# Delta net inversion: block masks laid on A instead of on its product, ScalarE evicting the product, and k, q, kb kept in the load's buffer

## Chip, cores and metric

One core of a Trainium2 chip runs the whole program once. The metric is the device time of that execution in microseconds; the median of several runs is compared.

## What is computed

One decoder layer: x (1024 tokens by 1024 features) is normed and projected; a gated delta net (4 heads of 128) and a sparse attention (8 heads of 64) run side by side, their outputs are merged, and a gated feed-forward part follows. All is float32. The change lies in the delta net, whose chunks need the inverse of a unit lower triangular matrix:

```python
kb = k * beta[..., None]
a_low = jnp.where(strict, jnp.einsum('bhnid,bhnjd->bhnij', kb, k) * decay, 0.0)
ia = a_low + jnp.eye(c, dtype=q.dtype)
u = lax.linalg.triangular_solve(ia, v * beta[..., None], left_side=True, lower=True, unit_diagonal=True)
w = lax.linalg.triangular_solve(ia, kb * jnp.exp(gc)[..., None], left_side=True, lower=True, unit_diagonal=True)
...
def step(state, inp):
    qk_n, qg_n, kd_n, u_n, w_n, gl_n = inp
    v_new = u_n - jnp.einsum('bhcd,bhde->bhce', w_n, state)
    o_n = jnp.einsum('bhcd,bhde->bhce', qg_n, state) + jnp.einsum('bhij,bhje->bhie', qk_n, v_new)
    state = state * gl_n[..., None, None] + jnp.einsum('bhcd,bhce->bhde', kd_n, v_new)
```

## The kernel before

The sequence is cut into 8 chunks of 128 tokens; a tile `[128, 4, 128]` holds one chunk for the 4 heads. After the projections to q, k, v (until some 205 us) four generators run woven into each other, with the remaining input projections as filler:

- `prepare_chunks` loads a chunk's q, k, v as `G` (line 506, SP's queue, one buffer) and the summed decays as `E` (line 509). TensorE transposes v, k and q (`pvt`, `pk`, `pqt`, lines 522, 530, 536). VectorE subtracts on `E` (line 513), GpSimd applies two selects to it (lines 514 and 516), ScalarE takes the exponential. GpSimd's `rr` (line 541) gives the norms, and VectorE scales to `kh` and `qh` (544, 546); GpSimd makes `kb` and `kd` and, in two products, `KQs` (helper `pmul`, line 89). TensorE transposes `kh`, `qh`, `kb` (555, 560, 565) and forms `pa` (580), from which VectorE makes `A` and `qkT` (583, 584). `A` goes to DRAM as `sq_a` (587) and comes back as 16x16 diagonal blocks `U` (591); VectorE inverts these in 15 small steps of a product `Ut` (596) and a sum `Yb` (598); they go to DRAM as `sq_y` (599) and come back as the block diagonal `Y` (601).
- `solve_chunks` widens the inverse three times, to blocks of 32, 64 and 128 (levels 4 to 6). A level transposes `Y` (`px`, 616), copies it to `X` (ScalarE, 617), forms `pp` from `A` and `X` (621), keeps only the off-diagonal blocks by multiplying with the mask `LM` (`Pm`, VectorE, 623), forms `py` (627) and subtracts it from `Y` (VectorE, 628).
- `scan_chunks` carries the state from chunk to chunk (`pr`, `pvn`, `pS`, `po`, `zt`), and `turn_chunks` transposes and splits its output (`at`, line 86).
- The filler is `projections`: three matmuls for each step (lines 147 to 149, `pn` and `pm`), evicted by ScalarE (`nst`, 710, two PSUM buffers).

`weave` picks the next piece by a small model of TensorE's time, in which each yield gives its cost and its delay. TensorE's instructions stay in that order by `manual_schedule`; on the other engines and the queues the framework's scheduler sets the order. The small tiles lie in a pool where a name has one buffer if no number is given: `gt("A", ..., 3)`, `gt("X", ...)`, `gt("Pm", ...)`.

Of the kernel before, what the change touches and what calls it, by code (L numbers as in the profile page):

```python
# [15 lines left out]
ALU = mybir.AluOpType  # L16
# [4 lines left out]
P = 128  # L21
# [4 lines left out]
H = 4  # L26
# [7 lines left out]
def tile_hybrid(ctx: ExitStack, tc: tile.TileContext, a: dict, out: bass.AP, dbg=None):  # L34
    nc = tc.nc
# [43 lines left out]
    def blocks(t):  # L79
        return bass.AP(tensor=t.tensor, offset=t.offset, ap=[[16 * P + 16, 32], [P, 16], [1, 16]])  # L80
# [7 lines left out]
    def pmul(out_, x, y):  # L88
        nc.gpsimd.tensor_tensor(out_, x, y, op=ALU.mult)
# [206 lines left out]
    def psB(name):  # L296
        return ps.tile([P, H, P], F32, tag="pb", name=name, bufs=3)
# [75 lines left out]
    def gt(name, shape, bufs=1, dt=F32):  # L373
        return gpool[0].tile(shape, dt, tag=name, name=name, bufs=bufs)
# [8 lines left out]
                            fill=0.0, base=0, channel_multiplier=-1)  # L383
# [5 lines left out]
    LM = gt("LM", [P, 3, P])  # L389
    for l in range(4, 7):  # L390
        b = 1 << l
        nb = P // (2 * b)
        v = LM[:, l - 4, :].rearrange("p (m s) -> p m s", s=2 * b)
        src = ones.rearrange("p (m s) -> p m s", s=2 * b)

        nc.gpsimd.affine_select(out=v, in_=src, pattern=[[-2 * b, nb], [0, 2 * b]], compare_op=ALU.is_ge,
                                fill=0.0, base=-b, channel_multiplier=1)

        nc.gpsimd.affine_select(out=v, in_=v, pattern=[[2 * b, nb], [0, 2 * b]], compare_op=ALU.is_gt,
                                fill=0.0, base=2 * b, channel_multiplier=-1)  # L400

        nc.gpsimd.affine_select(out=v, in_=v, pattern=[[0, nb], [-1, 2 * b]], compare_op=ALU.is_gt,
                                fill=0.0, base=b, channel_multiplier=0)
    Yb = [gt(f"Yb{i}", [32, 16, 16]) for i in range(2)]
    for i in range(2):
        nc.vector.memset(Yb[i], 0.0)
# [81 lines left out]
    def bc(ap, n=P):  # L488
        return ap[:, :, None].broadcast_to([P, ap.shape[1], n])

    def bc_h(ap):
        return ap[:, None, :].broadcast_to([P, H, P])
# [8 lines left out]
    def prepare_chunks():  # L501
        for c in range(NT):
            while c >= scanned[0] + 3:
                yield None
            G = gt("G", [P, 12, P])
# [9 lines left out]
                                    fill=NEG, base=0, channel_multiplier=-1)  # L515
            nc.gpsimd.affine_select(out=E, in_=E, pattern=[[0, H], [1, P]], compare_op=ALU.not_equal,
                                    fill=0.0, base=0, channel_multiplier=-1)
# [22 lines left out]
            rr = gt("rr", [P, 24], 2)[:, :8]  # L540
            nc.gpsimd.tensor_tensor(rr, ss, expo, op=ALU.pow)
            yield 230, 5000
            kh = gt("kh", [P, H, P])
            nc.vector.tensor_tensor(kh, pk, bc(rr[:, 0:4]), op=ALU.mult)
            qh = gt("qh", [P, H, P])
            nc.vector.tensor_tensor(qh, pq, bc(rr[:, 4:8]), op=ALU.mult)
            kb = gt("kb", [P, H, P])
            pmul(kb, kh, bc(beta[:, c, :]))
            yield 0, 3500

# [23 lines left out]
            A = gt("A", [P, H, P], 3)  # L574
            qkT = gt("qkT", [P, H, P], 3)
            for u in range(2):
                pa = psA("pa")
                pav = pa.rearrange("p (h u) i -> p h u i", h=2)
                for h in range(2):
                    nc.tensor.matmul(pav[:, h, :, :], khT[:, 2 * u + h, :], KQ[:, 2 * u + h, :, :],  # L580
                                     start=True, stop=True)
# [11 lines left out]
            for j in range(14, -1, -1):  # L593
# [3 lines left out]
                                        yb[:, j + 1:, j + 1:].rearrange("p b c -> p c b"), op=ALU.mult)  # L597
                nc.vector.tensor_reduce(yb[:, j, j + 1:], t[:, :n, :n], axis=AX.X, op=ALU.add, negate=True)
            nc.sync.dma_start(blocks(sq_y[c % 2]), yb)
# [6 lines left out]
    def solve_chunks():  # L606
        for c in range(NT):
            while begun[0] <= c:
                yield None
            yield 0, max(0.0, begun_at[c] + 21000 - m.t["pe"])  # L610
            A, Y = chunk[c][4], chunk[c][6]
            for l in range(4, 7):
                X = gt("X", [P, H, P])
                pt = psB("px")
                for h in range(H):
                    nc.tensor.transpose(pt[:, h, :], Y[:, h, :], ident)
                nc.scalar.copy(X, pt)
                yield 230, EV
                pp = psB("pp")
                for h in range(H):  # L620
                    nc.tensor.matmul(pp[:, h, :], A[:, h, :], X[:, h, :], start=True, stop=True)
                Pm = gt("Pm", [P, H, P])
                nc.vector.tensor_tensor(Pm, pp, bc_h(LM[:, l - 4, :]), op=ALU.mult)
                yield 880, EV
                py = psB("py")
                for h in range(H):
                    nc.tensor.matmul(py[:, h, :], Pm[:, h, :], Y[:, h, :], start=True, stop=True)
                nc.vector.tensor_tensor(Y, Y, py, op=ALU.subtract)
                yield 880, EV
            solved[0] = c + 1  # L630
# [97 lines left out]

    rest = projections()
    weave(m, [steps(m, g) for g in (scan_chunks(), turn_chunks(), solve_chunks(), prepare_chunks())], steps(m, rest))  # L730
    gd.close()

# [30 lines left out]
    for mask, pat, op, base, mult in ((maskD, -1, ALU.is_ge, 0, 1), (maskE, 1, ALU.is_gt, 0, -1),  # L763
# [3 lines left out]
                                channel_multiplier=mult)  # L767
# [5 lines left out]
                            fill=0.0, base=-31, channel_multiplier=1)  # L773
# [169 lines left out]
    with ExitStack() as ph:  # L943
        ap_ = pool(ph, "attn")

        def at_(name, shape, bufs=1, dt=F32):
            return ap_.tile(shape, dt, tag=name, name=name, bufs=bufs)
# [77 lines left out]
        def scores():  # L1025
            for u, (i, g, br, j0, nk) in enumerate(units):
# [10 lines left out]
                if br == 0:  # L1037
# [4 lines left out]
                    for h in range(4):  # L1042
                        for l in range(2):
                            nc.tensor.matmul(sv[:, h, :], qt[:, h, l, :], KCS[:, g, :], start=l == 0, stop=False)
                        nc.tensor.matmul(sv[:, h, :], identb, maskC[:, 56 - 8 * i:120 - 8 * i], start=False, stop=True)
                    nc.vector.tensor_reduce(mx[:, :, 0], sv, axis=AX.X, op=ALU.max, negate=True)
                    pr = at_("Pc", [P, 4, 64], 2)
# [7 lines left out]
                else:  # L1055
                    b = 0 if br == 1 else 1
                    cuts = (0, w) if nk <= 4 else (0, (nk + 1) // 2 * P, w)
                    for n in range(len(cuts) - 1):
# [7 lines left out]
                        for h in range(4):  # L1066
# [10 lines left out]
                            for e, (m0, mk) in enumerate(ext):  # L1077
                                nc.tensor.matmul(s[:, m0:m0 + P], identb, mk, start=False, stop=e == len(ext) - 1)  # L1078
                            nc.vector.tensor_reduce(mx[:, h, n:n + 1], s, axis=AX.X, op=ALU.max, negate=True)  # L1079
                            nc.scalar.activation(pr, s, AF.Exp, bias=mx[:, h, n:n + 1], accum_out=sums[:, h, n:n + 1])  # L1080
# [115 lines left out]
    A, Aop = {}, {}  # L1196
# [497 lines left out]
```

## Time and profile before

| | |
|---|---|
| median of 3 runs | 1787.52 us (1783.7 to 1788.48) |
| profiled execution | 1787.32 us |
| its span, first to last instruction | 1785.6 us |
| TensorE busy | 1717.4 us, 96% |
| VectorE busy | 1093.7 us, 61% |
| ScalarE busy | 767.2 us, 43% |
| GpSimd busy | 625.5 us, 35% |

The profile page gives busy time by engine and the span in 40 slices; the trace gives each instruction with its start, its length and what ended the idle time before it. PE is TensorE, PEld its weight loads, DVE is VectorE, ACT is ScalarE, POOL is GpSimd, SPq is SP's transfer queue. An idle time is put down to the instruction that came last. The woven stretch runs from about 225 to 510 us.

### The profile page before, as it was taken

The numbers are of one execution on the slowest core, as the hardware profiler recorded it, in microseconds if no ns is written. First come the engines' busy times: TensorE is split into PE (matmuls) and PEld (weight loads), VectorE is DVE, ScalarE is ACT, GpSimd is POOL, SyncE is SP. The second block draws the span as 40 slices with busy tenths as digits, with TensorE's granted clock in tenths as the row PEclk, the third lists the DMA queues.
The fourth block names the chain that finished last, engine by engine and source line by source line (L and its number), as shares of the span: only waits on it lengthen the run. The fifth ranks groups of instructions, "written<-read, shape, count | busy, mean of one in ns | idle before, by whom it ended". The sixth has DMA issues, their size and how long they took to land.

```text
span 1785.6 us, 25989 instructions
## 1 busy us (share of the span) xinstructions
PE 1717.4 (96%) x9348; PEld 1455.3 (82%) x9348; DVE 1093.7 (61%) x2062; ACT 767.2 (43%) x1806; POOL 625.5 (35%) x919
## 2 busy tenths in 40 slices
PE   7999988989999999999999999899999999999998
PEld 7888888989878777777878888688888888878886
DVE  6466556565534578677754434665555555588685
ACT  5244433343321598777742222433333333344452
POOL 3400143444131666667540220644435434200000
PEclk9999989999999999999999999999999999999999
DMA  6332443433364412011138360033333333482342
GB/s 209 95 101 95 144 118 108 111 100 100 94 173 141 112 42 54 22 48 36 51 108 249 114 212 1 12 119 107 100 95 121 103 99 112 161 306 88 98 139 100
DMA packets 183009, 196.39 MB, mean 110 GB/s; under 512 B 23409, under 2 KB 139361, under 8 KB 182881
## 3 DMA queue, kind: packets, MB, share of 16 engines
q1 hardware_dynamic: 164112, 162.03, 29.8%
q0 software_dynamic: 18560, 32.62, 6.1%
q8 instruction: 73, 1.20, 0.3%
q14 instruction: 56, 0.45, 0.1%
q10 hardware_dynamic: 208, 0.09, 0.0%
HBM read 139.01 MB, written 55.69 MB: 109 GB/s over the span
## 4 chain that ended last, share of the span: by engine, by line
PE 78%; issue 6%; DVE 6%; POOL 4%; ACT 2%; DMA 2%; POOLq 0%; SPq 0%; DVEq 0%; ACTq 0%
PE M L149 14%; PE M L148 14%; PE M L147 14%; PE ppt L1133 3%; PE s L1075 3%; PE pq L147 2%; PE pq L149 2%; PE pq L148 2%; PE po L1160 2%; PE pm L147 2%; PE pm L148 2%; PE pm L149 2%; PE po L1161 2%; DVE Ut L596 1%; PE pn L147 1%
## 5 line engine op out<-in xcount | busy, mean ns | idle before, releaser
L86 DVE TENSOR_TENSOR ptl<-ppt,pth 128x512 fp32r<-128x512 f32 (+1 forms) x148 | 98.8, 683 | 36.0 <-ACT pth L85 35.0
L1110 POOL TENSOR_SCALAR Ps<-Ps,cs 128x384 f32<-128x384 f32 (+3 forms) x192 | 112.3, 603 | 13.0 <-DVE cs L1088 6.0
L85 ACT ACTIVATE ahi<-fraw 128x512 fp32r<-128x512 f32 x88 | 55.6, 632 | 141.7 <-PE M L148 141.7
L1080 ACT ACTIVATE Ps<-s,mx 128x384 f32<-128x384 f32 (+3 forms) x192 | 106.5, 563 | 16.6 <-DVE mx L1079 15.6
L1079 DVE TENSOR_REDUCE mx<-s 128x1 f32<-128x384 f32 (+3 forms) x192 | 95.3, 514 | 22.8 <-PE s L1078 20.4
L1075 PE MATMUL s<-KT,qt 128*128 128x384 f32 (+3 forms) x384 | 100.4, 359 | 2.9 <-ACT Ps L1080 1.8
L147 PE MATMUL pn<-whi,h 128*128 128x264 f32 (+1 forms) x320 | 100.7, 315 | 0.0
L147 PE MATMUL pm<-h,whi 128*128 128x512 f32 x224 | 96.6, 431 | 0.8 <-ACT thm L725 0.7
L85 ACT ACTIVATE pth<-ppt 128x512 fp32r<-128x512 f32 (+1 forms) x148 | 86.2, 603 | 24.6 <-PE ppt L1133 23.6
L149 PE MATMUL pn<-whi,h 128*128 128x264 f32 (+1 forms) x320 | 91.6, 286 | 0.0
L148 PE MATMUL pn<-wlo,h 128*128 128x264 f32 (+1 forms) x320 | 91.5, 286 | 0.0
L149 PE MATMUL pm<-h,wlo 128*128 128x512 f32 x224 | 88.5, 395 | 0.0
L85 ACT ACTIVATE ahi<-fsum 128x512 fp32r<-128x512 f32 x66 | 41.7, 632 | 108.1 <-PE M L148 106.1
L148 PE MATMUL pm<-h,whi 128*128 128x512 f32 x224 | 88.1, 393 | 0.0
L86 DVE TENSOR_TENSOR wlo<-wraw,whi 128x1024 fp32r<-128x1024 f32 (+1 forms) x50 | 61.1, 1231 | 41.1 <-ACT whi L85 39.4
L86 DVE TENSOR_TENSOR alo<-fraw,ahi 128x512 fp32r<-128x512 f32 x88 | 70.5, 801 | 23.8 <-ACT ahi L85 23.8
L1617 POOL TENSOR_TENSOR rms_r<-rms_ms,small 128x1 f32<-128x1 f32 x8 | 5.1, 646 | 226.6 <-DVE rms_ms L1615 226.6
L1133 PE MATMUL ppt<-ident,Ps 128*128 128x128 f32 x528 | 77.7, 274 | 1.1 <-POOL Ps L1110 1.1
L147 PE MATMUL M<-act,ahi 128*128 128x512 f32 x194 | 76.1, 392 | 1.8 <-ACT act L85 1.8
L148 PE MATMUL M<-act,ahi 128*128 128x512 f32 x194 | 76.4, 394 | 0.3 <-DVE act L86 0.3
L149 PE MATMUL M<-act,alo 128*128 128x512 f32 x194 | 76.1, 392 | 0.0
L147 PE MATMUL pq<-h,whi 128*128 128x512 f32 x192 | 74.7, 389 | 0.0
(518 smaller groups left out, 5444.8 us busy)
## 6 DMA issues: line engine op xcount, KB each, us to landing
wraw<-in_w_in_dram SPq DMA_DIRECT2D x50, 512.0 KB, 4.4
fraw<-in_w_gate_up_dram SPq DMA_DIRECT2D x44, 512.0 KB, 4.2
ar<-act_d SPq DMA_DIRECT2D x35, 512.0 KB, 3.5
act_d<-asum SPq DMA_DIRECT2D x44, 256.0 KB, 2.4
act_d<-act SPq DMA_DIRECT2D x33, 256.0 KB, 2.0
gt_d<-thm POOLq DMA_DIRECT2D x32, 256.0 KB, 2.8
gg<-gt_d SPq DMA_DIRECT2D x32, 256.0 KB, 2.9
qkv_d<-ac POOLq DMA_DIRECT2D x24, 256.0 KB, 2.3
```

What stands on the lines that cost most here:

```text
L85: nc.scalar.activation(hi, src, AF.Copy)
L86: nc.vector.tensor_tensor(lo, src, hi.bitcast(F32), op=ALU.subtract)
L147: nc.tensor.matmul(ps, ah, bh, start=first, stop=False)
L148: nc.tensor.matmul(ps, ah, bl, start=False, stop=False)
L149: nc.tensor.matmul(ps, al, bh, start=False, stop=last)
L1075: nc.tensor.matmul(s, qt[:, h, l, :], KT[g][:, b, j0 * P + c0:j0 * P + c1], start=l == 0, stop=l == 1 and not ext)
L1079: nc.vector.tensor_reduce(mx[:, h, n:n + 1], s, axis=AX.X, op=ALU.max, negate=True)
L1080: nc.scalar.activation(pr, s, AF.Exp, bias=mx[:, h, n:n + 1], accum_out=sums[:, h, n:n + 1])
L1110: nc.gpsimd.tensor_scalar(v, v, cs[:, h, n:n + 1], 1.0, op0=ALU.mult, op1=ALU.mult)
L1133: nc.tensor.transpose(pt[:k, h, :], prs[h][:, jj * P:jj * P + k], ident)
L1160: nc.tensor.matmul(po, v, th_, start=first, stop=False)
L1161: nc.tensor.matmul(po, v, tl_, start=False, stop=fin is not None)
```

## The change

The mask tables `LM` are turned (the block rows and columns that they keep change places), and VectorE multiplies `A` by the mask into a new tile `Am` with two buffers at the head of each level. `pp` is formed from `Am`, and ScalarE copies it to `Pm`. `kh`, `qh` and `kb` lose their tiles and are written over q, k and v in `G`.

```diff
@@ the masks
-                                fill=0.0, base=-b, channel_multiplier=1)
+                                fill=0.0, base=0, channel_multiplier=1)
...
-                                fill=0.0, base=2 * b, channel_multiplier=-1)
-
-        nc.gpsimd.affine_select(out=v, in_=v, pattern=[[0, nb], [-1, 2 * b]], compare_op=ALU.is_gt,
-                                fill=0.0, base=b, channel_multiplier=0)
+                                fill=0.0, base=b, channel_multiplier=-1)
+
+        nc.gpsimd.affine_select(out=v, in_=v, pattern=[[0, nb], [1, 2 * b]], compare_op=ALU.is_ge,
+                                fill=0.0, base=-b, channel_multiplier=0)
@@ prepare_chunks
-            kh = gt("kh", [P, H, P])
+            kh, qh, kb = (G[:, 4 * j:4 * j + 4, :] for j in range(3))
             nc.vector.tensor_tensor(kh, pk, bc(rr[:, 0:4]), op=ALU.mult)
-            qh = gt("qh", [P, H, P])
             nc.vector.tensor_tensor(qh, pq, bc(rr[:, 4:8]), op=ALU.mult)
-            kb = gt("kb", [P, H, P])
             pmul(kb, kh, bc(beta[:, c, :]))
@@ solve_chunks
             for l in range(4, 7):
+                Am = gt("Am", [P, H, P], 2)
+                nc.vector.tensor_tensor(Am, A, bc_h(LM[:, l - 4, :]), op=ALU.mult)
                 X = gt("X", [P, H, P])
...
-                    nc.tensor.matmul(pp[:, h, :], A[:, h, :], X[:, h, :], start=True, stop=True)
+                    nc.tensor.matmul(pp[:, h, :], Am[:, h, :], X[:, h, :], start=True, stop=True)
                 Pm = gt("Pm", [P, H, P])
-                nc.vector.tensor_tensor(Pm, pp, bc_h(LM[:, l - 4, :]), op=ALU.mult)
+                nc.scalar.copy(Pm, pp)
```

TensorE's order is the same in both. On VectorE, the start of a chunk's small inversion (the stretch at 355 us of the trace). Before:

```order
L513 TENSOR_TENSOR E<-E,gc 128x512
L596 TENSOR_TENSOR Ut<-U,Yb_880 32x1
L598 TENSOR_REDUCE Yb_880<-Ut 32x1
L623 TENSOR_TENSOR Pm<-pp,LM 128x512
L596 TENSOR_TENSOR Ut<-U,Yb_880 32x2x2
L598 TENSOR_REDUCE Yb_880<-Ut 32x2
L596 TENSOR_TENSOR Ut<-U,Yb_880 32x3x3
```

And with the change (lines from 547 on stand two lower, so that 596 is 594):

```order
L513 TENSOR_TENSOR E<-E,gc 128x512
L594 TENSOR_TENSOR Ut<-U,Yb_880 32x1
L596 TENSOR_REDUCE Yb_880<-Ut 32x1
L612 TENSOR_TENSOR Am<-A,LM 128x512
L594 TENSOR_TENSOR Ut<-U,Yb_880 32x2x2
L596 TENSOR_REDUCE Yb_880<-Ut 32x2
L594 TENSOR_TENSOR Ut<-U,Yb_880 32x3x3
```

`Am` stands in the slot that `Pm` had; the first two `Am` of the program stand ahead, so each is the one of two levels later.

On VectorE, the end of the same small inversion (at 368 us). Before:

```order
L598 TENSOR_REDUCE Yb_880<-Ut 32x15
L539 SCALAR_TENSOR_TENSOR ss<-ss,rscale 128x8
L623 TENSOR_TENSOR Pm<-pp,LM 128x512
L544 TENSOR_TENSOR kh<-pk,rr 128x512
L546 TENSOR_TENSOR qh<-pqt,rr 128x512
L86 TENSOR_TENSOR at_3840<-pat,at_3839 128x512
L628 TENSOR_TENSOR Y<-Y,py 128x512
L623 TENSOR_TENSOR Pm<-pp,LM 128x512
```

With the change (`kh` and `qh` are now parts of `G`):

```order
L596 TENSOR_REDUCE Yb_880<-Ut 32x15
L539 SCALAR_TENSOR_TENSOR ss<-ss,rscale 128x8
L612 TENSOR_TENSOR Am<-A,LM 128x512
L544 TENSOR_TENSOR G<-pk,rr 128x512
L545 TENSOR_TENSOR G<-pqt,rr 128x512
L86 TENSOR_TENSOR at_3847<-pat,at_3846 128x512
L628 TENSOR_TENSOR Y<-Y,py 128x512
L612 TENSOR_TENSOR Am<-A,LM 128x512
```

`Am` again takes `Pm`'s place, and `Y` keeps its place behind `kh`, `qh` and `at`.

On SP's queue, around the load of a later chunk's `G` (at 381 to 394 us). Before:

```order
L587 DMA sq_a_106<-A 128x4x128
L509 DMA E<-gc_d 128x512
L591 DMA U<-sq_a_106 32x16x16
L506 DMA G<-qkv_d_73 128x12x128
L599 DMA sq_y_108<-Yb_880 32x16x16
L680 DMA zt<-z_d_77 128x512
L601 DMA Y<-sq_y_108 128x4x128
L587 DMA sq_a_107<-A 128x4x128
```

With the change:

```order
L589 DMA U<-sq_a_106 32x16x16
L597 DMA sq_y_108<-Yb_880 32x16x16
L680 DMA zt<-z_d_77 128x512
L599 DMA Y<-sq_y_108 128x4x128
L506 DMA G<-qkv_d_73 128x12x128
L585 DMA sq_a_107<-A 128x4x128
L509 DMA E<-gc_d 128x512
L589 DMA U<-sq_a_107 32x16x16
```

The load of `G` moves from behind `U` to in front of the next chunk's `sq_a` and `E`.

## Rows read from the trace of the kernel before

**Rows 1.** What TensorE waited for, 225 to 510 us: total us, times, longest.
```profile
PE py L627 <- DVE Pm L623: 11.3, 8, 2.2
PE px L616 <- DVE Y L628: 4.0, 4, 1.4
```
**Rows 2.** Groups by line, 225 to 510 us: busy us, mean ns, idle us before.
```profile
L623 DVE TENSOR_TENSOR Pm<-pp,LM 128x512 f32<-128x512 f32 x24 | 16.3, 679 | 30.7 <-PE pp L621 30.7
L513 DVE TENSOR_TENSOR E<-E,gc 128x512 f32<-128x512 f32 x7 | 4.8, 692 | 17.1 <-ACT sb L512 17.1
L617 ACT COPY X<-px 128x512 f32<-128x512 f32 x24 | 14.0, 584 | 54.0 <-PE px L616 53.8 <-ACT rv L651 0.2
```
**Rows 3.** Timeline of TensorE: start us, length us, instruction, idle before it.
```profile
258.44 1.12 PE L616 MATMUL px<-ident,Y 128*128 128x128 f32 x4 [0.74 <-DMA Y<-sq_y]
...
369.30 0.94 PE L627 MATMUL py<-Y,Pm 128*128 128x128 f32 x6 [2.15 <-DVE Pm L623]
...
372.97 0.66 PE L616 MATMUL px<-ident,Y 128*128 128x128 f32 x4 [0.72 <-DVE Y L628]
...
400.58 1.16 PE L627 MATMUL py<-Y,Pm 128*128 128x128 f32 x8 [1.98 <-DVE Pm L623]
...
431.18 1.05 PE L627 MATMUL py<-Y,Pm 128*128 128x128 f32 x7 [2.06 <-DVE Pm L623]
...
435.53 0.66 PE L616 MATMUL px<-ident,Y 128*128 128x128 f32 x4 [1.40 <-DVE Y L628]
```
**Rows 4.** Timeline of VectorE, end of a chunk's small inversion.
```profile
368.57 0.67 DVE L623 TENSOR_TENSOR Pm<-pp,LM 128x512 f32<-128x512 f32 x1
370.43 0.69 DVE L544 TENSOR_TENSOR kh<-pk,rr 128x512 f32<-128x512 f32 x1 [1.19 <-POOL rr L541]
...
372.24 0.68 DVE L628 TENSOR_TENSOR Y<-Y,py 128x512 f32<-128x512 f32 x1
```
**Rows 5.** Timeline of VectorE, beside GpSimd's selects.
```profile
324.71 0.46 DVE L596 TENSOR_TENSOR Ut<-U,Yb 32x4 f32<-32x4 f32 x1
...
355.93 0.67 DVE L623 TENSOR_TENSOR Pm<-pp,LM 128x512 f32<-128x512 f32 x1
```
**Rows 6.** Timeline of GpSimd, the same places and the two products.
```profile
324.52 0.63 POOL L514 TENSOR_SCALAR_AFFINE_SELECT E<-E 128x512 f32<-128x512 f32 x1 [4.41 <-DVE Ut L596]
...
355.84 0.64 POOL L514 TENSOR_SCALAR_AFFINE_SELECT E<-E 128x512 f32<-128x512 f32 x1 [1.60 <-DVE Ut L596]
356.54 0.64 POOL L516 TENSOR_SCALAR_AFFINE_SELECT E<-E 128x512 f32<-128x512 f32 x1
...
376.65 2.59 POOL L89 TENSOR_TENSOR KQs<-KQ,sb 128x512 f32<-128x512 f32 x2 [0.64 <-ACT KQ L561]
```
**Rows 7.** Timeline of VectorE beside those two products.
```profile
376.87 0.69 DVE L623 TENSOR_TENSOR Pm<-pp,LM 128x512 f32<-128x512 f32 x1 [3.96 <-PE pp L621]
379.25 0.42 DVE L583 TENSOR_TENSOR A<-pa,E 128x256 f32<-128x256 f32 x1 [1.69 <-PE pa L580]
```
**Rows 8.** The loads of G (line 506): from issue to landing.
```profile
DMA to landing us min/median/max: 4.7/5.1/6.5
```
**Rows 9.** Timeline of SP's queue.
```profile
381.46 0.36 SPq L587 DMA_DIRECT2D sq_a<-A  x1
```
**Rows 10.** Timeline of TensorE: transposes of kb, and the next chunk's first transposes.
```profile
226.90 0.60 PE L565 MATMUL pkb<-ident,kb 128*128 128x128 f32 x4
...
232.33 0.60 PE L522 MATMUL pvt<-ident,G 128*128 128x128 f32 x4
...
376.67 0.60 PE L565 MATMUL pkb<-ident,kb 128*128 128x128 f32 x4
```
**Rows 11.** Busy by stretch: sum, PE, PEld, DVE, ACT, POOL; granted clock, DMA share, GB/s.
```profile
366.00:370.00 4.00, 1.85 (x16) 1.64 (x15) 3.07 (x8) 0.97 (x2) 1.27 (x1) 1.00 0.51 136
724.00:728.00 4.00, 4.00 (x21) 3.39 (x19) 2.88 (x6) 2.54 (x9) 0.00 (x0) 0.61 0.27 70
```
**Rows 12.** Timeline of TensorE: the wait in front of that fall of the clock.
```profile
723.65 0.99 PE L1133 MATMUL ppt<-ident,Pc 128*64 128x128 f32 x4 [3.04 <-ACT Ps L1080]
```

## The prediction

> **What bounds it now.** I read the list of what each engine waited for, on TensorE, in the stretch 225 to 510 us, which holds everything that the change touches: outside it no instruction moves on any engine. The reader is to see that TensorE waited 11.3 us there for `Pm`, in eight places, and 4.0 us for `Y`, in four [rows 1]. The rest of the time it is fed by the projections that are woven between the steps, in an order that is fixed and that the change leaves as it is. So the change can give at most 11.3 us, and only where nothing else is late right behind.
>
> The timeline of TensorE shows those waits by place [rows 3]. Three chunks look alike: 2.15 us for `Pm` at 369.30 and 0.72 us for `Y` at 372.97; 1.98 us at 400.58, with `Y` just in time at the next step; 2.06 us at 431.18 and 1.40 us at 435.53. The timeline of VectorE says why [rows 4]. `Pm` starts at 368.57 because VectorE is in its own chain (the 15 small steps of the 16x16 inversion), not because it waits. `Y` starts at 372.24, some two microseconds after the product `py` of 369.30 is done: it stands in VectorE's queue behind `kh`, `qh` and `at`, and `kh` waits for GpSimd's `rr`. So in these chunks VectorE's chain is the bound and the wait for `Pm` is slack of the same chain, taken one step early.
>
> **The change, part by part.**
>
> *The mask moves from the product to A.* VectorE loses 24 products from PSUM of 0.679 us and gains 24 products `Am` with both inputs in SBUF; the nearest row is the subtraction on `E`, 0.692 us [rows 2]. VectorE's work is the same within 0.3 us. By the order, `Am` of two levels later stands in the very slot that `Pm` had, and since `Am` has two buffers it also waits for the same product `pp`. VectorE's chain is not shortened by anything.
>
> *ScalarE gets 24 copies.* Each is priced by the copy to `X`, 0.584 us [rows 2]; ScalarE sits idle 53.8 us before those alone, so 14 us of copies hide. If that cover were gone, the copies of `pn` queued behind would hold TensorE's two buffers; I cost it at nothing. The eight waits at `py` go: -11.3 us. What is late next is `Y`. In the three chunks above 2.15, 1.98 and 2.06 us come back at `px`, and so does most of the 1.14 us of a fourth. Of the early four (3.97 us together) two stand in front of steps where TensorE had no wait; there I take **-1.5 us**, bounds 0 and -4.0.
>
> *Am against GpSimd.* GpSimd's select at 324.52 lasts 0.63 us; VectorE's 32x4 product with both inputs in SBUF that began at 324.71 took 0.46 us and ended with it. `Pm`, with one input in PSUM, began at 355.93 inside the select of 355.84 and took its usual 0.67 us [rows 5, 6]. So `Am` in `Pm`'s slot must wait until 356.48, which is 0.55 us, and it then keeps out, or is followed by, the second select of 0.64 us that the next small products meet: 0.55 to 1.2 us, and I take 0.9. There are three such slots: **+2.7 us** (0 if the two do not exclude each other, 3.6 at most). The Trainium skill states this as a rule, in "SBUF — State Buffer", section "Who interferes with whom": a VectorE instruction with two SBUF inputs and a GpSimd instruction that reads SBUF exclude each other for the whole instruction, whichever starts second being fully blocked. By that rule the trace agrees (0.46 us, ending with the select), the price would be the upper 1.2 us, and the sum 0.9 us higher.
>
> The same three chunks have a second slot: `Pm` at 376.87 lies inside GpSimd's two products `KQs`, 376.65 to 379.24 [rows 6, 7]. `Am` would come out at 379.24 and push `A`, which VectorE issued at 379.25, by up to 0.69 us; part of that lies under the wait for the second `pa`. I take 0.3 each: **+0.9 us** (0 to 2.1).
>
> *k, q and kb in G's place.* `G` has one buffer, so the next load now waits for the transposes of `kb` and the product `kd` instead of the transposes of q. For the second chunk that is 227.50 (226.90 and 0.60); with a landing of 5.1 us it is there at 232.6, and `pvt` wants it at 232.33 [rows 8, 10]: **+0.3 us** (0 to 1.7, with the slowest landing, 6.5). In the later chunks the load goes out at about 377.3 (end of `kb`'s transposes) and lands at 382.4, while `sq_a` and `E`, on which the next inversion waits, go out from 381.46 on [rows 8 to 10]. They share the transfer engines for up to 0.9 us: three times 0.4, about half of it, **+1.2 us** (0 to 2.7). And SP's order now puts the first `Y` behind `sq_a` and `E`; the first `px` waited 0.74 us for that load already [rows 3]. No row has this order. Below nothing, above half a landing, 2.4 us; I take **+1.0 us**, nearer to the wait there is.
>
> *The clock.* Where `py` no longer waits, the two waits of a chunk become one. With what is lost above in such a chunk (0.9 + 0.3 + 0.4 = 1.6 us) they are 2.87 + 1.6 = 4.5 us, 1.98 + 1.6 = 3.6 us and 3.46 + 1.6 = 5.1 us long. After a wait of 3.04 us at 723.65 the granted clock was 0.61 over 724 to 728, so half the time at the lower level: 0.39 of 4 us is 1.56 us. Over 366 to 370, with the wait of 2.15 us inside, it stayed at 1.00 [rows 3, 11, 12]. The steps behind (`px` to `pa`) are on the loop, so I count 1.5 us for each of the three: **+4.5 us** (0 to 4.7).
>
> **Sum.** -1.5 + 2.7 + 0.9 + 0.3 + 1.2 + 1.0 + 4.5 = +9.1 us against the profiled execution, 1787.3 us: **1796.4 us**. The median of the runs shown is 1787.5, so the sum stands for it as it is. With every term at its lower end it is 1783.3, at its upper 1804.5.
>
> **Rivals.** (1) *The waits only change place.* If `Am` and GpSimd don't hold each other and the longer wait leaves the clock alone, what is left is -1.5 + 0.3 + 1.2 + 1.0 = +1.0 us, 1788.3. For it: the clock held over 2.15 us, and no row shows a full-size VectorE product with two SBUF inputs beside GpSimd. Against it: the 0.46 us. (2) *The waits go and don't come back*: faster, 1787.3 - 11.3 = 1776.0. This needs `Y` to start right after `py`. It decides if VectorE reaches `Y` within a microsecond of `py`'s end; in the rows it comes some two microseconds later, behind work that the change leaves there. Against it stands also that `Am` waits for `pp` in `Pm`'s slot. (3) *The load of G is late in every chunk*: seven waits of 0.3 to 1.7 us on top of the forecast, 1799 to 1806. Against it: only the second and third chunk's `pvt` follow the load closely.
>
> **Chances.** About 0.3% (5.4 us) is what a measurement of this kernel can tell from no change, so slower is above 1792.9 and faster below 1782.1. Forecast 0.45 and rival (3) 0.05, both slower: 0.50. Rival (1), the same: 0.37. Rival (2): 0.13. The range goes from 1785, which takes in rival (1) with a microsecond or two of gain, to 1805, the upper ends of all terms; outside lie rival (2) and a part of (3). Slower and same hold most of the chance; the likeliest case alone reaches from 1793 to 1805.
>
> **What would show it.** Right: no wait of TensorE for `Pm` over half a microsecond, the waits for `Y` up from 4.0 to above 12 us, `Am` of 1.2 us and longer in the slots behind `E`, and a granted clock below 1 within 370 to 380, 400 to 412 or 432 to 444. The first `pvt` after the moved load waits for a DMA. Wrong: waits for `Y` that stay near 4 us mean that VectorE's chain was not the bound; `Am` of 0.69 us throughout takes out 3.6 us and most of the clock's 4.5.

## Result and profile after

The changed kernel takes 1795.47 us (median of 6, 1793.14 to 1801.96) against 1787.03 us (median of 6): 1.0054 of the time before, with an interval of 1.0042 to 1.0066. That is 8.4 us slower by the medians (9.7 by the ratio); 1796.4 was forecast, within 1785 to 1805. The profiled execution is the slowest of the six: 1801.96 us, span 1800.0 us, mean granted clock 0.984 (before: 1785.6 us and 0.993). At the end of the woven stretch it is 9.7 us behind the profiled execution of before; 4.7 us more are lost later, in code that the change leaves alone, and the other five executions are 3 to 9 us shorter. So stages are read from this trace, and sizes from the medians.

The list of what TensorE waited for, 225 to 520 us (total us, times, longest), to be held against [rows 1]:

```profile
PE px L616 <- DVE Y L628: 13.0, 6, 4.1
PE px L616 <- DMA Y<-sq_y: 3.1, 1, 3.1
...
PE pvn L649 <- DVE Y L628: 1.9, 1, 1.9
...
PE pvt L522 <- DMA G<-qkv_d: 0.6, 1, 0.6
PE py L627 <- ACT Pm L623: 0.4, 1, 0.4
```

The 11.3 us of waits for `Pm` have shrunk to 0.4, and the waits for `Y` have grown from 4.0 to 13.0 us. TensorE's timeline shows where; the two waits of a chunk in [rows 3] have become one in three late chunks:

```profile
251.11 0.63 PE L522 MATMUL pvt<-ident,G 128*128 128x128 f32 x4 [0.62 <-DMA G<-qkv_d]
261.48 1.12 PE L616 MATMUL px<-ident,Y 128*128 128x128 f32 x4 [3.11 <-DMA Y<-sq_y]
374.33 1.11 PE L616 MATMUL px<-ident,Y 128*128 128x128 f32 x4 [3.88 <-DVE Y L628]
409.31 0.66 PE L616 MATMUL px<-ident,Y 128*128 128x128 f32 x4 [3.28 <-DVE Y L628]
443.44 1.12 PE L616 MATMUL px<-ident,Y 128*128 128x128 f32 x4 [4.12 <-DVE Y L628]
```

VectorE's timeline in front of the wait at 374.33, and the longest `Am`, show what makes `Y` late, as [rows 4] did before:

```profile
344.85 3.26 DVE L612 TENSOR_TENSOR Am<-A,LM 128x512 f32<-128x512 f32 x1 [1.85 <-PE pp L621]
356.20 1.09 DVE L612 TENSOR_TENSOR Am<-A,LM 128x512 f32<-128x512 f32 x1
369.56 0.67 DVE L612 TENSOR_TENSOR Am<-A,LM 128x512 f32<-128x512 f32 x1
371.80 0.69 DVE L544 TENSOR_TENSOR G<-pk,rr 128x512 f32<-128x512 f32 x1 [1.57 <-POOL rr L541]
372.40 0.68 DVE L545 TENSOR_TENSOR G<-pqt,rr 128x512 f32<-128x512 f32 x1
373.00 0.68 DVE L86 TENSOR_TENSOR at<-pat,at 128x512 fp32r<-128x512 f32 x1
373.60 0.68 DVE L628 TENSOR_TENSOR Y<-Y,py 128x512 f32<-128x512 f32 x1
```

`py` ran from 367.61 to 368.66 and `Y` begins at 373.60, still behind `kh` and `qh` (here `G`) and `at`. GpSimd's timeline at the same places, against [rows 6]:

```profile
345.04 2.52 POOL L89 TENSOR_TENSOR KQs<-KQ,sb 128x512 f32<-128x512 f32 x2
356.11 0.64 POOL L514 TENSOR_SCALAR_AFFINE_SELECT E<-E 128x512 f32<-128x512 f32 x1 [2.44 <-DVE Ut L594]
356.81 0.97 POOL L516 TENSOR_SCALAR_AFFINE_SELECT E<-E 128x512 f32<-128x512 f32 x1
369.72 2.05 POOL L541 TENSOR_TENSOR rr<-ss,small 128x8 f32<-128x8 f32 x1 [4.15 <-DVE ss L539]
```

`Am` at 356.20 takes 1.09 us instead of 0.67, the second select 0.97 instead of 0.64 [rows 6]; `rr`, beside the `Am` of 369.56, takes 2.05 us, where the other seven take 1.66 or 1.67; and an `Am` beside the two products `KQs` takes 3.26 us.

So the delay of this chunk can be followed step by step. VectorE's subtraction on `E`, at the head of the chunk's small inversion, and TensorE's `py` after the wait, before and with the change:

```profile
355.07 0.69 DVE L513 TENSOR_TENSOR E<-E,gc 128x512 f32<-128x512 f32 x1 [2.87 <-ACT sb L512]
379.05 1.05 PE L627 MATMUL py<-Y,Pm 128*128 128x128 f32 x8
...
355.35 0.69 DVE L513 TENSOR_TENSOR E<-E,gc 128x512 f32<-128x512 f32 x1 [3.71 <-ACT sb L512]
383.01 1.05 PE L627 MATMUL py<-Y,Pm 128*128 128x128 f32 x8
```

The subtraction is 0.28 us later. The product at the end of the small inversion (`Pm` at 368.57, `Am` at 369.56) is 0.99 us later: 0.71 more, all of it beside the two selects. `kh` is 1.37 us later (370.43, 371.80): 0.38 more, by the longer `rr`. `Y` and `px` are 1.36 us later (`px` 372.97, 374.33). `py` is 3.96 us later: 2.60 more, at the lower clock shown below. Over all 24 `Am` (groups by line, 225 to 510 us: busy us, mean ns, idle us before), with ScalarE's copies:

```profile
L612 DVE TENSOR_TENSOR Am<-A,LM 128x512 f32<-128x512 f32 x24 | 24.5, 1023 | 32.0 <-PE pp L621 32.0
L623 ACT COPY Pm<-pp 128x512 f32<-128x512 f32 x24 | 14.1, 586 | 12.8 <-PE pp L621 12.8
```

The mean `Am` is 1.02 us, half as long again as the product that it replaces [rows 2]. Last the clock, by stretch (columns as [rows 11]) around the waits at 374.33 and 443.44:

```profile
370.00:374.00 4.00, 0.46 (x4) 0.25 (x3) 2.43 (x5) 0.00 (x0) 3.14 (x3) 0.89 0.57 139
374.00:380.00 6.00, 5.67 (x27) 5.67 (x28) 0.28 (x1) 1.79 (x4) 3.43 (x5) 0.50 0.65 134
...
440.00:444.00 4.00, 0.56 (x3) 0.56 (x4) 2.48 (x4) 0.00 (x0) 2.67 (x3) 0.68 0.82 196
444.00:448.00 4.00, 4.00 (x21) 4.00 (x20) 0.00 (x0) 1.17 (x2) 2.41 (x3) 0.50 0.47 98
```

During and after the waits of 3.88 and 4.12 us the clock stands at 0.50, the lower of its two levels (1.2 GHz), while TensorE has full work; in the profiled execution of before, none of these three chunks showed anything below 1.00.

### The profile page after: what moved, and what is told of

The parts are those of the page before. It is cut to its first block, busy times and chain, and to the rows that moved or that the text cites. A ratio compares the mean times of both kernels' runs of the same rounds, so it can differ in the third digit from the quotient of the medians.

```text
span 1800.0 us, 26026 instructions
## 1 busy us (share of the span) xinstructions
PE 1730.1 (96%) x9348; PEld 1467.4 (82%) x9348; DVE 1102.8 (61%) x2062; ACT 779.1 (43%) x1830; POOL 626.7 (35%) x919
## 4 chain that ended last, share of the span: by engine, by line
PE 66%; issue 5%; POOL 3%; DVE 3%; ACT 2%; DMA 1%; POOLq 0%; DVEq 0%; ACTq 0%; SPq 0%
PE M L149 14%; PE M L148 14%; PE M L147 14%; PE ppt L1133 3%; PE s L1075 3%; PE po L1160 2%; PE pm L147 2%; PE pm L149 2%; PE pm L148 2%; PE po L1161 2%; PE dn L149 1%; PE dn L147 1%; PE dn L148 1%; POOL Ps L1110 1%; PE dn L1362 1%
## 5 line engine op out<-in xcount | busy, mean ns | idle before, releaser
L85 ACT ACTIVATE ahi<-ar 128x512 fp32r<-128x512 f32 x66 | 41.4, 629 | 77.0 <-PE M L148 41.6
```

The costliest lines, as they stand in the source:

```text
L85: nc.scalar.activation(hi, src, AF.Copy)
```

## Experiments

Each kernel was timed against the kernel before on its own chip; ratios carry their 95% intervals. Differences in us between two kernels below are differences of their ratios times 1787.

| kernel | median us | ratio to before | interval |
|---|---|---|---|
| changed kernel | 1795.47 | 1.0054 | 1.0042 to 1.0066 |
| g_alone | 1781.92 | 0.9974 | 0.9960 to 0.9988 |
| g_pad | 1786.51 | 0.9994 | 0.9983 to 1.0004 |
| mask_alone | 1796.84 | 1.0054 | 1.0037 to 1.0071 |
| fill_wait | 1792.81 | 1.0038 | 1.0025 to 1.0050 |
| y_first | 1784.51 | 0.9991 | 0.9980 to 1.0002 |
| y_first_before | 1785.75 | 0.9994 | 0.9985 to 1.0003 |
| am_act | 1794.23 | 1.0043 | 1.0031 to 1.0055 |
| am_act2 | 1791.35 | 1.0019 | 1.0008 to 1.0029 |
| am_act_yfirst | 1780.95 | 0.9963 | 0.9949 to 0.9977 |
| old_masks | 1780.59 | 0.9961 | 0.9947 to 0.9974 |
| best | 1772.26 | 0.9912 | 0.9899 to 0.9925 |

### The two halves of the change

**g_alone**, the place of k, q and kb alone:

```diff
 # the kernel before
-            kh = gt("kh", [P, H, P])
+            kh, qh, kb = (G[:, 4 * j:4 * j + 4, :] for j in range(3))
...
-            qh = gt("qh", [P, H, P])
...
-            kb = gt("kb", [P, H, P])
```

> The kernel before with one part of the change alone: k, q and kb are written into G, the masks stay on the products. Theory A (what the prediction says of the loads): the loads that go out later cost 0.3 + 1.2 + 1.0 = 2.5 us, the eight waits for Pm stay as they are (11.3 us), no clock fall at 374, 411 and 443: about 1789.5 us, between 1787 and 1792. Rival B (the loads are the whole loss, 2.4 us more wait for the first Y and the longer time at the low clock behind it): 1793 to 1796. If the loads cost nothing: 1787.

None of these: 0.9974, a gain of 4.6 us. In the profiled execution the stage itself ends 0.6 us later than before. The gain comes behind it, at the first step of the next stage. The kernel before, TensorE and SP's queue:

```profile
530.86 0.20 PE L823 MATMUL ppos<-ident,posr 16*128 16x16 f32 x1 [3.08 <-DMA posr<-in_cmp_pos_k_dram]
...
527.06 0.59 SPq L810 DMA_DIRECT2D posr<-in_cmp_pos_k_dram  x1
```

In g_alone, SP's queue:

```profile
517.53 0.60 SPq L808 DMA_DIRECT2D posr<-in_cmp_pos_k_dram  x1
```

The load goes out 9.5 us earlier, and the wait is gone. What SP's queue waited for in the kernel before, 500 to 540 us, says why; in g_alone this line is missing:

```profile
SPq L752 <- DMA at_d<-at: 12.0, 2, 11.0
```

The pool of the small tiles is 6 KB per partition smaller, so the new stage's first tiles no longer lie where `at` was still being stored. The changed kernel gives 4 of the 6 KB to `Am` and has the wait again (3.3 us). To see whether that is all:

**g_pad**, g_alone with those 4 KB filled:

```diff
+            if c == 0:
+                pad = gt("fill", [P, 8, P])
+                nc.gpsimd.memset(pad[:, 0, 0:1], 0.0)
```

> The kernel g_alone with a tile of 4 KB per partition more in the same pool, the size that Am takes in the changed kernel; one element of it is written once. Theory: g_alone was faster than before by some 4 us only because the smaller pool let the first loads of the next stage (the tables once and the position table posr) go out 10 us earlier, so that TensorE's wait of 3.1 us for posr at 531 fell away; with the pool filled up that wait is back and the time is 1785 to 1788 us. Rival (the gain is in the chunks themselves, k, q and kb in G's place are worth 4 us): 1781 to 1783, and no wait for posr.

0.9994, and the wait for `posr` is back, at 3.4 us, with 11.9 us of SP's queue waiting for the stores of `at`. So the place of k, q and kb is worth nothing that can be measured inside the stage (-1.1 us, -3.0 to +0.7), although both delays that I priced are there: over 225 to 545 us g_pad's list has

```profile
PE py L628 <- DVE Pm L624: 9.3, 6, 2.4
PE px L617 <- DMA Y<-sq_y: 4.4, 1, 4.4
PE ppos L824 <- DMA posr<-in_cmp_pos_k_dram: 3.4, 1, 3.4
...
PE pvt L522 <- DMA G<-qkv_d: 1.6, 2, 1.4
...
PE px L617 <- DVE Y L629: 1.4, 2, 1.0
```

The later first `Y` is given back: the waits at 266.01, 269.87 and 278.04 of the kernel before (0.24, 0.87 and 1.40 us) are not in g_pad's trace: TensorE comes later to these steps, and at the third of them VectorE has `Pm` under way at 275.41, where it was 277.32.

**mask_alone**, the other half:

```diff
 # the changed kernel
-            kh, qh, kb = (G[:, 4 * j:4 * j + 4, :] for j in range(3))
+            kh = gt("kh", [P, H, P])
...
+            qh = gt("qh", [P, H, P])
...
+            kb = gt("kb", [P, H, P])
...
-                Am = gt("Am", [P, H, P], 2)
+                Am = gt("Am", [P, H, P])
...
-                Pm = gt("Pm", [P, H, P])
+                Pm = X
```

> The changed kernel with k, q and kb in tiles of their own again; so that they fit, Am has one buffer and Pm is written over X. Theory A: all but the 2.5 us of the loads stays: TensorE waits above 10 us for Y, none for Pm, the clock falls in the three late chunks: about 1793 us, 1791 to 1796. Rival B (the loads are the loss): 1787 or below. Rival C (masks and ScalarE copies give a gain that the loads ate): 1776 to 1783.

1.0054, as much as the changed kernel, and with g_pad at nothing: the loss is in the masks and the copies. The median, 1796.84 us, lies above the range of theory A, which had the right picture and put too little on it. What TensorE waited for, 225 to 545 us:

```profile
PE px L618 <- DVE Y L630: 14.1, 8, 4.1
...
PE pp L623 <- ACT X L619: 2.4, 2, 1.8
```

mask_alone also gives `Am` one buffer instead of two and writes `Pm` over `X`. The wait for `X` is 1.4 us longer than in the changed kernel (2.4 for 1.0) and the one for `Pm`, here in `X`, 0.8 us longer (1.2 for 0.4), so a part of the 9.7 us may be its own.

### The clock

**fill_wait**, work for TensorE inside the three long waits:

```diff
                 pt = psB("px")
+                if l == 6 and c in (3, 4, 5):
+                    hx = hT2[1][0]
+                    for _ in range(14):
+                        nc.tensor.matmul(pt.rearrange("p h k -> p (h k)"), hx[:, 0, 0:P], hx[:, 0, :],
+                                         start=True, stop=True)
```

> The changed kernel with 14 extra products of 128x512 (some 3.0 us at full clock) in front of the px that waited 3.88, 3.28 and 4.12 us for Y; their result is overwritten, so the output stays. They lie inside the waits. Theory A: the granted clock stays at 1.00 in the three stretches, and the steps behind px come sooner by 1.5 to 2.6 us each: 1788 to 1791 us. Rival (the clock is innocent, since VectorE's and GpSimd's chain sets the pace in these stretches): the clock holds and the time stays at 1795 to 1796.

Timeline of TensorE and stretches in fill_wait:

```profile
372.58 3.36 PE L618 MATMUL px<-h 128*128 128x512 f32 x14
376.63 0.66 PE L621 MATMUL px<-ident,Y 128*128 128x128 f32 x4 [0.69 <-DVE Y L633]
...
374.00:380.00 6.00, 5.31 (x39) 4.65 (x38) 2.48 (x4) 1.92 (x4) 4.79 (x7) 1.00 0.86 197
```

The clock holds at 1.00 in all three chunks. From `px` to `py` TensorE then takes 6.06 us in each, as in the kernel before (6.08, 6.06, 6.06); in the changed kernel's trace it took 8.68, 7.67 and 8.28. So the low clock cost 6.4 us in that execution, the longest of the six. By the ratios 2.9 us are gone (1.0054 to 1.0038), and since the two intervals overlap, that is anything from nothing to some 6 us. The clock is a part of the loss; its size is not settled. By the ratio 6.8 us are still lost with a full clock, since `Y` comes as late as in the changed kernel.

A merged wait is not needed for such a fall. In four kernels with the masks as before (g_alone, g_pad, y_first_before, old_masks) it came behind the single wait for `Pm`, of 2.26 to 2.50 us, in the first of these chunks; in y_first_before (columns as [rows 11]):

```profile
366.00:372.00 6.00, 4.49 (x25) 4.49 (x26) 3.90 (x8) 0.00 (x0) 4.89 (x6) 0.72 0.52 130
```

It did not come each time: behind 2.42 us for `Pm` in the third chunk the clock fell in g_pad and not in g_alone.

### The place of Y in VectorE's queue

**y_first** pins `kh` and `qh` behind the last `Y`, by an order without a wait:

```diff
+    def behind(i):
+        if lastY:
+            tc.add_manual_dep(i.ins, lastY[-1].ins.name, mybir.DependencyInfo(
+                mybir.DependencyClass.NoSync, mybir.DependencyReason.DATA))
...
-            nc.vector.tensor_tensor(kh, pk, bc(rr[:, 0:4]), op=ALU.mult)
+            behind(nc.vector.tensor_tensor(kh, pk, bc(rr[:, 0:4]), op=ALU.mult))
-            nc.vector.tensor_tensor(qh, pq, bc(rr[:, 4:8]), op=ALU.mult)
+            behind(nc.vector.tensor_tensor(qh, pq, bc(rr[:, 4:8]), op=ALU.mult))
...
-                nc.vector.tensor_tensor(Y, Y, py, op=ALU.subtract)
+                lastY.append(nc.vector.tensor_tensor(Y, Y, py, op=ALU.subtract))
```

> The changed kernel, but on VectorE kh and qh stand behind the subtraction that makes Y (three chunks change their order, the others stay). Theory A (Y comes late because of its place in VectorE's queue, not because of py): Y starts at about 370.9, 407 and 439.9 instead of 373.6, 408.6 and 442.7, the three waits shrink from 11.3 us to about 4, the clock holds, and the time is 1780 to 1785 us, below the kernel before. Rival (kh and qh, which come later, hold the transposes of k and q and so the next chunk by as much): 1793 to 1796.

0.9991, 11.3 us less than the changed kernel. Its waits for `Y` over 225 to 545 us:

```profile
PE px L623 <- DVE Y L635: 5.5, 6, 1.8
```

The three late ones are 1.01, 1.80 and 1.01 us, about the 4 us expected. VectorE and TensorE in y_first, at the place of the fence above:

```profile
370.13 0.67 DVE L86 TENSOR_TENSOR at<-pat,at 128x512 fp32r<-128x512 f32 x1
370.74 0.67 DVE L635 TENSOR_TENSOR Y<-Y,py 128x512 f32<-128x512 f32 x1
371.78 0.69 DVE L551 TENSOR_TENSOR G<-pk,rr 128x512 f32<-128x512 f32 x1 [0.38 <-POOL rr L548]
...
371.45 0.66 PE L623 MATMUL px<-ident,Y 128*128 128x128 f32 x4 [1.01 <-DVE Y L635]
```

`Y` starts 2.86 us sooner, in time in which VectorE had stood idle for `rr`; `kh` starts at 371.78, where it was at 371.80. The order cost the changed kernel a wait for nothing.

**y_first_before** is the same order in the kernel before:

> The kernel before with kh and qh behind Y in VectorE's queue, nothing else. Theory A: in two late chunks Y starts 1.5 to 2 us earlier, but the waits for Pm (2.15, 1.98, 2.06 us) stay, since Pm is in VectorE's chain ahead of it: 1782 to 1786. If this order alone is worth as much as in y_first (11 us): 1776, and the masks' place would not matter.

0.9994 (-1.1 us, -2.7 to +0.5). The waits for `Pm` stay, because `Pm` is in VectorE's chain itself:

```profile
PE py L634 <- DVE Pm L630: 9.9, 7, 2.5
```

In these two kernels the order pays only where the product of `pp` is evicted by another engine.

### Am off VectorE

**am_act** has ScalarE copy the blocks that the mask keeps, into tiles that are zeroed once:

```diff
+    Ams = [gt(f"Am{i}", [P, H, P]) for i in range(3)]
+    for t in Ams:
+        nc.gpsimd.memset(t, 0.0)
...
-                Am = gt("Am", [P, H, P], 2)
-                nc.vector.tensor_tensor(Am, A, bc_h(LM[:, l - 4, :]), op=ALU.mult)
+                Am, b = Ams[l - 4], 1 << l
+                for r0 in range(0, P, 2 * b):
+                    nc.scalar.copy(Am[r0:r0 + b, :, r0 + b:r0 + 2 * b], A[r0:r0 + b, :, r0 + b:r0 + 2 * b])
```

> The changed kernel with the masked A made by ScalarE: seven small copies per chunk of the blocks that the mask keeps, into three tiles that are zeroed once; VectorE has no Am at all. Theory A (Am beside GpSimd's work is what makes Y later than before, about 1 us in each late chunk, and the clock multiplies it): without Am the waits for Y in the three late chunks fall from 11.3 us to 6 to 8 us, and the time is 1783 to 1789. Rival (the loss comes from the two waits of a chunk being made one, wherever Am is computed, or from ScalarE's copies): 1793 to 1797, or more with 56 further copies on ScalarE.

1.0043, a miss. The median, 1794.23 us, lies where the rival said, but the trace shows a reason that I had not thought of. What TensorE waited for in am_act, 195 to 240 us, and SP's queue:

```profile
PE pvt L522 <- DMA G<-qkv_d: 4.7, 2, 2.8
...
213.01 0.37 SPq L506 DMA_DIRECT2D G<-qkv_d  x1
```

The three tiles stood first in the pool and moved `G` to a place that came free later: its first load goes out at 213.01 instead of the changed kernel's 208.53. **am_act2** allocates them when the first level begins, behind the other tiles.

> am_act again, with its three tiles placed behind the others in the pool: in am_act they stood first, and the first load of G, whose place then came free later, was issued 4.4 us later (the whole of the stage began 4.4 us late). Theory A (two parts: Am beside GpSimd's work, and the merged wait with its clock): the stage begins on time, and from 318 to 442 us of the kernel before it loses about 4 us, as in am_act, instead of 10.6: 1788 to 1791 us. Rival (the late start was made good inside the stage anyway, so that the loss comes from the merged waits alone): 1793 to 1796.

1.0019, by the median (1791.35 us) just above the upper edge of what was expected. In am_act2 `rr` takes 1.67 us at 369.53; the three waits for `Y` are 2.79, 3.69 and 2.80 us, and the clock falls behind the middle one alone. So taking `Am` off VectorE is worth 6.3 us of the changed kernel's loss, its share of the clock included. How much of that is the standing aside for GpSimd and how much VectorE's shorter queue was not separated.

**am_act_yfirst**, both together, with am_act's late start:

> am_act and y_first together: no Am on VectorE, and kh and qh behind Y in VectorE's queue. Theory A: the two gains are of the same waits and so add in part: the waits for Y shrink to 2 us or less, no clock fall in the late chunks, 1776 to 1783 us, below before by 0.2 to 0.6%. Rival (kh and qh, behind Y, become the next thing that TensorE waits for): 1784 to 1788.

0.9963, as expected.

### A version that beats both

**best** is am_act2 with y_first's order, and the two tiles `at` reserved early, so that the next stage's first tiles lie elsewhere:

```diff
             if c == 0:
+                for i in range(2):
+                    nc.gpsimd.memset(gt(f"at{i}", [P, H, P], 1, F32R)[:, 0, 0:1].bitcast(F32), 0.0)
```

> am_act2 with kh and qh behind Y in VectorE's queue, and the two tiles at reserved early in the pool, so that the first loads of the next stage no longer wait for the last stores of at. Theory: each cost that the runs named is taken away: no Am on VectorE, Y not behind kh and qh, no wait of 3.1 to 3.5 us for posr: 1773 to 1778 us. If the posr wait is hidden by something else: 1778 to 1781.

0.9912, 15 us below the kernel before by the medians and a little under the range expected. What its TensorE waited for, 225 to 545 us:

```profile
PE pk L537 <- DVE qkT L589: 3.2, 1, 3.2
PE px L632 <- DMA Y<-sq_y: 2.9, 1, 2.9
PE px L632 <- DVE Y L644: 2.1, 4, 1.0
```

13.0 us for `Y` have become 2.1, and `posr` is not in the list. **old_masks** is best with the masks as before (`Pm` by VectorE from `pp`, no `Am`):

> The kernel best with the masks as in the kernel before: VectorE multiplies pp by the mask, no Am; k, q and kb in G, kh and qh behind Y, and the early place of the tiles at stay. If the masked A and ScalarE's copies are worth something once Y stands first and Am is off VectorE: 1778 to 1783 us, some 6 to 10 us above best. Rival (best owes its gain to the order and the freed load alone): 1771 to 1775.

0.9961, as expected. The masked A with copies by ScalarE is worth 8.8 us (0.9961 to 0.9912, intervals apart), once `Am` is off VectorE and `Y` first; its three tiles also make best's pool larger, but neither kernel waits for `posr`. With the `Am` and the order of the change, the same idea cost 9.7.

## Why the prediction held, step by step

- *What bounds it.* That VectorE's chain, not the wait for `Pm`, sets the late chunks was right: the waits came back at `px`, 13.0 us of them where "above 12 us" was said. y_first shows the cause directly: with `Y` ahead of `kh` and `qh` the three late waits fall from 11.3 to 3.8 us.
- *The early gain, -1.5 us.* No run shows it. Between the steps at 269.87 and 303.32 the changed kernel gains 2.6 us on the profiled execution of before, but g_pad, which has the same loads and the old masks, gains 2.4, and y_first_before, which has the old masks and loads there, 1.8. In the profiled execution of before, VectorE waited 2.35 us for the load of `U` at 286.82; in y_first_before it waited 0.51, and TensorE's wait for `Pm` at 288 was not there.
- *ScalarE's copies, costed at nothing.* Right: from 225 to 520 us no `pn` waited for its eviction.
- *Am against GpSimd, +2.7 and +0.9 us.* Right in its mechanism, less so in its sizes. The three slots beside the selects took 1.09 to 1.10 us, not the 1.2 and longer given as a sign. From the start of `E` to the first `Y` behind it, VectorE took 6.42, 6.42 and 6.43 us for 5.73, 5.72 and 5.99: 0.7, 0.7 and 0.4 us where 0.9 each was forecast. The slots beside `KQs` cost nothing: `Am` took 1.41, 1.27 and 1.61 us there, and `A` still starts 1.06 to 1.07 us behind `pa`. The 3.26 us lie in a slot that the prediction did not name, though `Pm` at 345.42 had lain between the same products, and there `A` comes 1.88 us behind `pa` instead of 1.06. The Trainium skill's rule ("SBUF — State Buffer", "Who interferes with whom") is that a VectorE instruction with two SBUF inputs and a GpSimd instruction that reads SBUF exclude each other, and that the order of issue decides which one is blocked. The trace agrees with 1.09, 0.97 and 2.05 us in place of 0.67, 0.64 and 1.67, each for the one that starts second; the 3.26 us do not fit by recorded starts, since that `Am` begins 0.19 us before the products (344.85, 345.04) and ends 0.55 us after them. Not foreseen was the case of `rr`: 0.38 us more, in front of `kh` and so of `Y`. It is there at the same place in mask_alone, fill_wait and y_first, and not in am_act2, which has no `Am` on VectorE.
- *The loads, +2.5 us.* This is the step that failed: "+0.3", "+1.2" and "+1.0" were -1.1 us together (-3.0 to +0.7) in g_pad. The delays exist (the first `px` 2.4 us later in g_pad, more than my whole 1.0), but they fall where TensorE waited for VectorE a few steps on anyway. I had asked what hides a cost for ScalarE's copies, and not for the loads.
- *The clock, +4.5 us.* It fell in the three chunks named. Its cost is not settled: 2.9 us by the ratio of fill_wait, with an error as large, and 6.4 in the profiled execution, above the bound of 4.7. The reading it rests on had two faults. 0.61 over 4 us between levels of 0.5 and 1.0 is some three quarters of the time at the lower one, not half (the loss of 1.56 us is right). And the 1.00 behind 2.15 us was one execution; the four kernels above fell behind a wait hardly longer.
- *The sum.* 8.4 us by the medians for 9.1. That it is so close is partly luck: the loads were put 3.6 us too high by g_pad (2.5 for -1.1), and the masks, the copies and the clock 3.1 too low by mask_alone (6.6 for 9.7, a part of which may be its own). That the first step of the next stage would be touched through the pool was not considered; in the changed kernel it came to nothing (3.3 us of waiting against 3.1).
- *Rivals.* "The waits only change place" (1788.3 us) needed `Am` at its usual length and a full clock; the 1.09 us, the clock at 0.50 and the time speak against it. "The waits go" needed `Y` right behind `py`, and where that holds (y_first, best) the time does fall. Late loads of `G` in every chunk were not seen: `pvt` waited once for one, 0.62 us. (That rival's time was added up too low: seven waits of 0.3 to 1.7 us on 1796.4 reach 1808.)

## What to carry to other kernels

Before a wait is taken out, see what stands in its engine's queue between the awaited result and the next one that the same engine owes: if it is late for its own reasons, the wait moves one step on, and two short waits can become one long one, here with a fall of the clock behind it. A product moved to another place on an engine meets new neighbours on the others; look there for what it shares with them. And the size and order of tiles in a pool decide when the first loads of the stages around go out: test such edits with the pool held at its size, as g_pad did.

## What the runs showed that was not expected

- 14 products of 128x512 inside a wait (3.36 us) kept the clock at 1.00 in three places where it had fallen to 0.50.
- 6 KB less in a pool sent the next stage's first load out 9.5 us earlier and removed a wait of 3.1 us; 6 KB put in front of the other tiles delayed the first load of their own stage by 4.5 us (am_act, 213.01 against 208.53 in the changed kernel).
- GpSimd's `rr`, on 8 elements per partition, took 2.05 us where a VectorE product with two SBUF inputs ran beside it, and at most 1.67 us the other seven times in the changed kernel.
- The clock also fell behind single waits of 2.26 to 2.50 us, in four kernels, and not behind one of 2.15 us or another of 2.42.
